# A four-layer hybrid decoder trunk on one core: order and engine of the work around the gated recurrence, and the compressed keys by token half

## The chip, the core and the metric

The program runs on one core of a Trainium2 chip. The profile names its engines PE (TensorE: matmuls; PEld is its weight load), DVE (VectorE), ACT (ScalarE), POOL (GpSimd) and SP (SyncE, which here only issues the weight DMAs). Each engine works through its own list of instructions in the order in which the built program has them; an instruction whose operands another engine makes waits on that engine. The metric is the device time of one execution in microseconds (us); the time of a kernel is the median of its runs.

## What is computed

Abridged to the two functions that the change touches. Four layers, 256 tokens of width 1024, float32. Layer 0 and 3 mix tokens by windowed attention, layer 1 by a gated linear recurrence, layer 2 by latent attention (MLA); each layer then attends to a memory and applies a gated MLP. The change touches layers 1 and 2:

```python
def rglru_block(x, w_in, conv_w, conv_b, w_rgate, b_rgate, w_igate, b_igate, lam, w_o):
    gate, u = jnp.split(x @ w_in, 2, axis=-1)
    u = causal_depthwise_conv(u, conv_w, conv_b)
    r = sigmoid(blockwise(u, w_rgate) + b_rgate)
    i = sigmoid(blockwise(u, w_igate) + b_igate)
    log_a = -LRU_C * r * softplus(-lam)
    a = jnp.exp(log_a)
    b_in = jnp.sqrt(-jnp.expm1(2.0 * log_a)) * (i * u)
    h = scan(h[t] = a[t] * h[t-1] + b_in[t])
    return (h * jax.nn.gelu(gate)) @ w_o

def mla_attention(x, w_down, q_norm, kv_norm, w_uq, w_ukv, w_o, cos_r, sin_r):
    c = x @ w_down
    cq, ckv, k_rope = jnp.split(c, [384, 640], axis=-1)
    cq, ckv = rms_norm(cq, q_norm), rms_norm(ckv, kv_norm)
    ...
```

## The kernel before

**Precision.** Every float32 product of a projection is made of three matmuls: `hi*hi + hi*lo + lo*hi` (`mm3`). So each weight piece has to be split on the chip: ACT casts a 128x512 part of the raw piece to `whi` (L287), then `wlo = raw - whi` is subtracted on DVE (L288). A piece is up to 128x2048, in parts of 512 columns, four parts to a full piece. `Weights` keeps three raw pieces (their 1 MB DMAs are issued by SP) and four split ones; `tick`, called from `bulk` after each matmul, issues a split every 1200 ns of matmul time, so that splits of later pieces lie beside the matmuls of earlier ones. Activations are split in the same way by `split` (L377 on ACT, L378 on DVE).

**Order.** A token string such as `RG_SEQ` says in which order the pieces of a layer are written; `play` walks it. In `rglru` the channels stand in four blocks of 256. Per block `b`: `a`/`b` project u, `V` is the convolution (L1173 on ACT, L1175 on DVE, tile `uc`) and the split into `uu`, `A` the two gate products and their tanh and exp (tiles `tt`, `av`, `ti`), `R` a product on DVE (L852), `g`/`h` project the gate. `Z` is one square root over `tt` of all four blocks on ACT (L885, 128x2048). `E` is the recurrence: a product (L856) and two scans of 128x256 (L858), all on DVE. `Y` is GELU on ACT (L863), its product with the state on DVE (L864), and the split into `oh`, `ol`. `C` is one chunk of the output projection: twelve matmuls of 512 columns on the four banks `y`, two chunks to a block; `G` loads the norm's weights through POOL's DMA queue into slots that `uu` leaves. `finish` makes the last four chunks, one output bank after the other, and the norm between them; the transposes of its result (`turn`, L366) and the splits `xh`, `xl` feed the next layer part.

The strings give the order of writing; the final order on each engine is made by the tile framework's scheduler, which takes the written order as priority and puts what it takes to be ready first. `tc.issue_after(ins)` lets an instruction stand no earlier than `ins`; `tc.high_priority()` lifts what is written inside.

**MLA.** `a_phase` projects the 384 query columns of both token halves (`s`), and through `more` the first half (512 of 1024 input rows) of the 320 key columns (`pk[s]`). `D` (`dk`) adds the second half of the input rows, `M` (`rms`) normalises (0, 1: queries of half 0, 1; 2, 3: keys), `U` (`c_turn`) transposes `cn` and splits it to `cqh`, `cql`.

Of the kernel before, what the change touches and what calls it, by code (L numbers as in the profile page):

```python
# [33 lines left out]
for _i in range(DEPTH):  # L34
    PHASES += [(("swa", "rglru", "mla")[_i % 3], _i), ("cross", _i), ("ffn", _i)]
SWA_SEQ = ("Q0 R0 Q1 R1 K0 U0 A2 S0 U1 B2 R2 S1 A3 N0 U2 B3 R3 N1 T0 S2 P0 U3 T1 S3 P1 C0 N2 C1 W0 T2 N3 C2 P2 T3 D3 "
           "P3 E3 G0")
RG_SEQ = ("a2 t0 b2 V1 a3 V0 V2 b3 A1 V3 g0 h0 A2 g2 A0 g1 A3 R3 R2 R0 R1 h1 Z0 E0 g3 E1 h3 Y0 C0 G0 h2 E2 E3 "
          "C1 Y1 C2 Y2 Y3 W0 C3")
MLA_SEQ = ("D1 M1 U0 M2 f1 M3 Q0 U1 K0 q0 f0 k0 v0 n0 q1 n2 v3 v1 r0 v2 n1 r1 S0 n3 S2 f2 N0 N1 f3 T0 T1 S4 N2 N3 P0 P1 G0 T2 "  # L40
           "T3 S6 N4 N5 P2 P3 T4 C0 T5 W0 N6 C1 P4 N7 T6 P5 C2 T7 P6 C3 P7")
X_SEQ = ("a2 t0 L1 b2 L0 L2 S0 a3 S1 N0 S2 T0 G0 N1 b3 T1 N2 P0 T2 L3 S3 N3 P1 W0 C0 C1 P2 T3 C2 P3 C3")

# [198 lines left out]
class Weights:  # L242


    def __init__(self, tc, pool, w):
        self.tc, self.nc, self.pool, self.w = tc, tc.nc, pool, w
        self.after = ()
        self.n_dma = self.n_split = self.n_done = 0
        self.part = 0
        self.raw, self.tiles, self.done, self.uses, self.late = {}, {}, set(), {}, []  # L250
        self.ns = 0.0
        self.hold = False
        self.then = {}

    def load(self):
# [15 lines left out]
    def step(self):  # L271
        k = self.n_split
        if k >= len(PLAN) or k - self.n_done >= NSPLIT:
            return False
        while self.n_dma <= k:
            self.load()
        n = PLAN[k][1]
        if self.part == 0:
            self.tiles[k] = (self.pool.tile([P, 2048], F32R, tag="whi", name="whi", bufs=NSPLIT),
                             self.pool.tile([P, 2048], F32R, tag="wlo", name="wlo", bufs=NSPLIT))  # L280
        hi, lo = self.tiles[k]
        c = slice(self.part, FIRST[k][self.part] if k < len(FIRST) else min(n, self.part + PART))
        raw = self.raw[k]
        with ExitStack() as st:
            for ins in self.after:
                st.enter_context(self.tc.issue_after(ins))
            self.nc.scalar.copy(out=hi[:, c], in_=raw[:, c])  # L287
            self.nc.vector.tensor_tensor(out=lo[:, c], in0=raw[:, c], in1=hi[:, c].bitcast(F32), op=ALU.subtract)  # L288
        self.part = c.stop
        if self.part >= n:  # L290
            self.part = 0
            del self.raw[k]
            self.n_split += 1
            self.load()
        return True
# [46 lines left out]
def trunk(ctx, tc, x_in, xT_in, memT_in, w, par, con, sinks, ln_g, ln_b, out):  # L342
    nc = tc.nc
    V, A, T = nc.vector, nc.scalar, nc.tensor
# [65 lines left out]
    def xs(kc, s=slice(0, 2)):  # L410
        return xh[:, s, kc], xl[:, s, kc]
# [401 lines left out]
    def rglru(mx, i, rest):  # L813
# [39 lines left out]

        def recur(b):
            t = tt[:, b]
            V.tensor_tensor(out=t, in0=t, in1=us[b][0], op=ALU.mult)  # L856
            for c in range(2):
                V.tensor_tensor_scan(out=t[:, c], data0=av[:, b, c], data1=t[:, c], initial=0.0, op0=ALU.mult, op1=ALU.add)  # L858

        def gated(b):  # L860
            ge = mx.tile([P, 2, S], F32, tag="ti", name="ge", bufs=2)
            with tc.issue_after(sq[0]):
                last[0] = A.activation(out=ge, in_=pgs.pop(b), func=AF.Gelu_apprx_tanh)  # L863
            V.tensor_tensor(out=ge, in0=ge, in1=tt[:, b], op=ALU.mult)  # L864
            oh = mx.tile([P, 2, S], F32R, tag="oh", name="oh", bufs=3)
            ol = mx.tile([P, 2, S], F32R, tag="ol", name="ol", bufs=3)
            split(oh, ol, ge)
            acts[b] = [(oh[:, c], ol[:, c]) for c in range(2)]

        op = OutProj(("mo", i), KC)  # L870
        pus, us, pgs, acts, last, sq, norm = {}, {}, {}, {}, [None], [None], [None]
        go = a_turn(mx, a_phase(("ua", i), 512, rest))

        def turned(_):
# [7 lines left out]
            return f  # L882

        def root(_):
            sq[0] = ins_of(A.activation(out=tt, in_=tt, func=AF.Sqrt, scale=0.25))  # L885

        def gb(_):
            norm[0] = Norm(op.y, mx, "uu", 3, i, 0)
# [2 lines left out]
                      "g": proj("ga", 0, pgs), "h": proj("ga", 1, pgs), "R": rate, "Z": root, "E": recur, "Y": gated,  # L891
                      "C": lambda ci: op.chunk(ci, acts[ci // 2][ci % 2]), "G": gb, "W": lambda _: want_sqrt(last[0])})
        norm[0].y = op.y
        return op.finish(acts[2] + acts[3], norm[0])


    def mla(mx, i, rest):
# [28 lines left out]
        pk = pcs[1]  # L926
# [381 lines left out]
```

## Time and profile before

| | before |
|---|---|
| time, median of 3 runs | 1379.81 us (1378.87 to 1380.73) |
| the profiled execution: its own time | 1378.62 us |
| the profiled execution: span from first to last instruction | 1376.8 us |
| PE busy, share of the span | 1362.9 us, 99% |
| DVE / ACT / POOL busy | 1084.4 / 881.4 / 13.0 us |
| granted TensorE clock, mean | 0.999 of full speed |

The window of layer 1's recurrence is about 386 to 475 us of the span, that of the head of MLA about 710 to 735 us. A row of the timeline reads: start in us, length in us, engine, line, operation, tiles out<-in, shapes, count, and in brackets the idle time of the engine just before it and what ended that. Matmuls overlap: one of 256 columns lasts 0.28 us in the rows and the next starts about 0.12 us after it; one of 512 columns lasts 0.39 and the next starts 0.23 us after it. So lost PE time is read from starts, not from lengths.

### The profile page before, as it was taken

The numbers are of one execution on the slowest core, as the hardware profiler recorded it, in microseconds if no ns is written. First come the engines' busy times: TensorE is split into PE (matmuls) and PEld (weight loads), VectorE is DVE, ScalarE is ACT, GpSimd is POOL, SyncE is SP. The second block draws the span as 40 slices with busy tenths as digits, with TensorE's granted clock in tenths as the row PEclk, the third lists the DMA queues.
The fourth block names the chain that finished last, engine by engine and source line by source line (L and its number), as shares of the span: only waits on it lengthen the run. The fifth ranks groups of instructions, "written<-read, shape, count | busy, mean of one in ns | idle before, by whom it ended". The sixth has DMA issues, their size and how long they took to land.

```text
span 1376.8 us, 23811 instructions
## 1 busy us (share of the span) xinstructions
PE 1362.9 (99%) x9122; PEld 1231.5 (89%) x9122; DVE 1084.4 (79%) x2397; ACT 881.4 (64%) x1896; POOL 13.0 (1%) x28
## 2 busy tenths in 40 slices
PE   9999999999999999999999999999999999999997
PEld 7987989999898898999988898999998879899996
DVE  6896879777888868877788686977779977897775
ACT  6675757555589667655557674855565866675553
POOL 0000000000000000000000000000000000000000
PEclk9999999999999999999999999999999999999999
DMA  9733536555435554555526442555554326455540
GB/s 334 278 118 123 214 130 237 184 187 191 174 137 197 202 175 177 214 187 194 186 86 237 154 181 95 218 211 191 191 196 145 136 109 228 153 214 189 189 174 31
DMA packets 40449, 246.78 MB, mean 179 GB/s; under 512 B 4496, under 2 KB 6800, under 8 KB 13712
## 3 DMA queue, kind: packets, MB, share of 16 engines
q1 hardware_dynamic: 36736, 232.56, 46.1%
q0 software_dynamic: 3456, 12.58, 2.7%
q8 instruction: 71, 1.16, 0.3%
q14 instruction: 42, 0.34, 0.1%
q10 hardware_dynamic: 144, 0.13, 0.0%
HBM read 244.21 MB, written 1.05 MB: 178 GB/s over the span
## 4 chain that ended last, share of the span: by engine, by line
PE 95%; DVE 3%; ACT 2%; DMA 0%; issue 0%; SPq 0%; DVEq 0%; ACTq 0%
PE ps L359 90%; PE ps L366 4%; PE ps L645 1%; ACT p L754 1%; DMA raw<-in_w_dram 0%; DVE wlo L288 0%; DVE tt L858 0%; DVE p L745 0%; DVE x L485 0%; ACT whi L287 0%; DVE x L487 0%; DVE x L461 0%; DVE tt L856 0%; ACT tt L885 0%; ACT xh L377 0%
## 5 line engine op out<-in xcount | busy, mean ns | idle before, releaser
L288 DVE TENSOR_TENSOR wlo<-raw,whi 128x512 fp32r<-128x512 f32 (+1 forms) x870 | 559.6, 683 | 144.6 <-ACT whi L287 138.1
L287 ACT CAST whi<-raw 128x512 fp32r<-128x512 f32 (+1 forms) x870 | 486.1, 619 | 165.3 <-PE ps L359 145.6
L359 PE MATMUL ps<-xh,whi 128*128 128x256 f32 x1504 | 421.2, 280 | 0.0
L359 PE MATMUL ps<-xh,wlo 128*128 128x256 f32 x1504 | 420.1, 279 | 0.0
L359 PE MATMUL ps<-xl,whi 128*128 128x256 f32 x1504 | 419.8, 279 | 0.0
L359 PEld LDWEIGHTS ps<-xl,whi 128*128 128x128 f32 x1504 | 282.7, 188 | 1.9
L359 PEld LDWEIGHTS ps<-xh,whi 128*128 128x128 f32 x1504 | 282.7, 188 | 1.8
L359 PEld LDWEIGHTS ps<-xh,wlo 128*128 128x128 f32 x1504 | 282.6, 188 | 0.0
L1175 DVE SCALAR_TENSOR_TENSOR cv<-ps,part,cv 128x255 f32<-128x255 f32 (+1 forms) x352 | 166.4, 477 | 3.8 <-ACT cv L1173 1.4
L359 PE MATMUL ps<-whi,xh 128*128 128x512 f32 (+3 forms) x336 | 118.8, 354 | 0.4 <-ACT xh L377 0.2
L359 PE MATMUL ps<-wlo,gh 128*128 128x512 f32 x352 | 116.0, 396 | 0.0
L359 PE MATMUL ps<-whi,gh 128*128 128x512 f32 x352 | 115.9, 396 | 0.0
L359 PE MATMUL ps<-wlo,xh 128*128 128x512 f32 (+3 forms) x336 | 115.7, 345 | 0.0
L359 PE MATMUL ps<-whi,gl 128*128 128x512 f32 x352 | 115.1, 393 | 0.0
L1173 ACT ACTIVATE cv<-ps,part 128x256 f32<-128x256 f32 x176 | 98.3, 563 | 16.9 <-DVE cv L1175 5.5
L377 ACT CAST gh<-cv 128x256 fp32r<-128x256 f32 x88 | 35.7, 406 | 107.6 <-DVE cv L1190 107.6
L359 PE MATMUL ps<-whi,oh 128*128 128x512 f32 x256 | 92.8, 402 | 1.9 <-ACT oh L377 1.9
L359 PE MATMUL ps<-whi,xl 128*128 128x512 f32 (+3 forms) x336 | 92.6, 347 | 0.0
L359 PE MATMUL ps<-whi,ol 128*128 128x512 f32 x256 | 90.6, 394 | 0.0
L359 PE MATMUL ps<-wlo,oh 128*128 128x512 f32 x256 | 90.2, 393 | 0.0
L359 PEld LDWEIGHTS ps<-whi,gl 128*128 128x128 f32 x352 | 66.3, 188 | 15.8
L359 PEld LDWEIGHTS ps<-wlo,gh 128*128 128x128 f32 x352 | 66.4, 189 | 15.3
(230 smaller groups left out, 1843.1 us busy)
## 6 DMA issues: line engine op xcount, KB each, us to landing
raw<-in_w_dram SPq DMA_DIRECT2D x208, 1024.0 KB, 4.8
lng<-in_ln_g_dram POOLq DMA_DIRECT2D x12, 512.0 KB, 4.0
lnb<-in_ln_b_dram POOLq DMA_DIRECT2D x12, 512.0 KB, 5.7
raw<-in_w_dram SPq DMA_DIRECT2D x15, 256.0 KB, 5.4
raw<-in_w_dram SPq DMA_DIRECT2D x5, 768.0 KB, 4.2
raw<-in_w_dram SPq DMA_DIRECT2D x2, 640.0 KB, 4.2
xf<-in_xT_dram SPq DMA_DIRECT2D x1, 1024.0 KB, 8.8
x<-in_x_dram SPq DMA_DIRECT2D x1, 1024.0 KB, 15.3
```

The costliest lines, as they stand in the source:

```text
L287: self.nc.scalar.copy(out=hi[:, c], in_=raw[:, c])
L288: self.nc.vector.tensor_tensor(out=lo[:, c], in0=raw[:, c], in1=hi[:, c].bitcast(F32), op=ALU.subtract)
L359: T.matmul(o, lhsT=l, rhs=r, start=st, stop=sp, **kw)
L366: T.transpose(o, i, ident)
L377: a = A.copy(out=hi, in_=src)
L645: T.matmul(o, lhsT=l, rhs=r, start=st, stop=sp, skip_group_check=True)
L754: last[0] = A.activation(out=pr[:, hd], in_=pr[:, hd], func=AF.Exp, scale=A_D ** -0.5, bias=nm[:, b, hd:hd + 1], accum_out=sm[:, b, hd:hd ...
L1173: A.activation(out=dst, in_=src, func=AF.Identity, scale=wc[:, taps - 1:taps], bias=bias)
L1175: V.scalar_tensor_tensor(out=dst[:, d:], in0=src[:, :S - d], scalar=wc[:, taps - 1 - d:taps - d], in1=dst[:, d:], op0=ALU.mult, op1=ALU.add)
```

## The change

1. `RG_SEQ`: `Z` stands before the four `R` instead of behind them, `Y0` right behind `E0`, `Y1` behind `E1`.
2. `recur` for blocks 0 and 1, `gated` for blocks 0 and 1 and the square root are written inside `tc.high_priority()`; and the product that begins `recur(b)` may not stand before the product of `gated(b - 1)` (for blocks 2 and 3: of `gated(1)`).
3. While `W.spare` is set (from the first token of the recurrence's string to its last), the subtraction of the second and the fourth part of a weight piece is issued to POOL instead of DVE. These are 20 subtractions of ten pieces.
4. `MLA_SEQ`: `D1` (both token halves) becomes `D0` before the transposes of the queries and `D1` behind them; `dk(s)` does one token half.

```diff
-RG_SEQ = ("a2 t0 b2 V1 a3 V0 V2 b3 A1 V3 g0 h0 A2 g2 A0 g1 A3 R3 R2 R0 R1 h1 Z0 E0 g3 E1 h3 Y0 C0 G0 h2 E2 E3 "
-          "C1 Y1 C2 Y2 Y3 W0 C3")
-MLA_SEQ = ("D1 M1 U0 M2 f1 M3 Q0 U1 K0 q0 ...
+RG_SEQ = ("a2 t0 b2 V1 a3 V0 V2 b3 A1 V3 g0 h0 A2 g2 A0 g1 A3 Z0 R3 R2 R0 R1 h1 E0 Y0 g3 E1 h3 Y1 C0 G0 h2 E2 E3 "
+          "C1 C2 Y2 Y3 W0 C3")
+MLA_SEQ = ("M1 D0 U0 M2 D1 f1 M3 Q0 U1 K0 q0 ...
...
-            self.nc.vector.tensor_tensor(out=lo[:, c], in0=raw[:, c], in1=hi[:, c].bitcast(F32), op=ALU.subtract)
+            eng = self.nc.gpsimd if self.spare and c.start in (512, 1536) else self.nc.vector
+            eng.tensor_tensor(out=lo[:, c], in0=raw[:, c], in1=hi[:, c].bitcast(F32), op=ALU.subtract)
...
         def recur(b):
             t = tt[:, b]
-            V.tensor_tensor(out=t, in0=t, in1=us[b][0], op=ALU.mult)
-            for c in range(2):
-                V.tensor_tensor_scan(...)
+            with ExitStack() as hp:
+                if b < 2:
+                    hp.enter_context(tc.high_priority())
+                with ExitStack() as st:
+                    if b:
+                        st.enter_context(tc.issue_after(gm[min(b - 1, 1)]))
+                    V.tensor_tensor(out=t, in0=t, in1=us[b][0], op=ALU.mult)
+                for c in range(2):
+                    V.tensor_tensor_scan(...)
...
+            with ExitStack() as st:
+                if b < 2:
+                    st.enter_context(tc.high_priority())
...
+                gm[b] = ins_of(V.tensor_tensor(out=ge, in0=ge, in1=tt[:, b], op=ALU.mult))
...
         def root(_):
-            sq[0] = ins_of(A.activation(out=tt, in_=tt, func=AF.Sqrt, scale=0.25))
+            with tc.high_priority():
+                sq[0] = ins_of(A.activation(out=tt, in_=tt, func=AF.Sqrt, scale=0.25))
...
-        def dk(_):
+        def dk(s):
             wt = W.get((("dk", i), 1))
             for k in range(4):
-                for s in range(2):
-                    mm3(pk[s][:, :nk], xs(4 + k, s), [t[:, nk * k:nk * k + nk] for t in wt], False, k == 3, bulk)
-            W.free((("dk", i), 1))
+                mm3(pk[s][:, :nk], xs(4 + k, s), [t[:, nk * k:nk * k + nk] for t in wt], False, k == 3, bulk)
+            if s == 1:
+                W.free((("dk", i), 1))
```

How the instructions then stand, at three places.

**Place 1, ACT and DVE, from the last gates of the recurrence (`ti_4797`, block 3) on.** On ACT, before, the four weight casts stand ahead of the square root:

```order
L847 ACTIVATE ti_4797<-ps_4784,hb_76 128x256 x2
L287 CAST whi_4806<-raw_4654 128x512 x4
L885 ACT_TABLE_LOAD
L885 ACTIVATE tt_4236<-tt_4236 128x2048
L863 ACT_TABLE_LOAD
L863 ACTIVATE ge_4897<-ps_4546 128x512
L287 CAST whi_4957<-raw_4727 128x512 x3
L377 CAST oh_4900<-ge_4897 128x512
```

The second tanh and the casts are done when the square root's table load begins. On ACT now, from the first of the two tanh of that block:

```order
L849 ACTIVATE ti_4797<-ps_4784,hb_76 128x256
L898 ACT_TABLE_LOAD
L898 ACTIVATE tt_4236<-tt_4236 128x2048
L874 ACT_TABLE_LOAD
L874 ACTIVATE ge_4845<-ps_4546 128x512
L849 ACTIVATE ti_4797<-ps_4784,hb_76 128x256
L288 CAST whi_4807<-raw_4654 128x512
L379 CAST oh_4848<-ge_4845 128x512
L288 CAST whi_4807<-raw_4654 128x512 x2
L874 ACTIVATE ge_4904<-ps_4716 128x512
```

The square root has moved ahead of the second tanh and of four weight casts (`whi_4806` before, `whi_4807` now: the weights of the first output chunks); these casts now stand behind the first GELU. On DVE, before, from the first product of the recurrence:

```order
L856 TENSOR_TENSOR tt_4236<-tt_4236,uc_4434 128x512
L856 TENSOR_TENSOR tt_4236<-tt_4236,uc_4393 128x512
L858 SCALAR_TENSOR_TENSOR tt_4236<-av_4237,tt_4236 128x256 x4
L864 TENSOR_TENSOR ge_4897<-ge_4897,tt_4236 128x512
L856 TENSOR_TENSOR tt_4236<-tt_4236,uc_4446 128x512
L856 TENSOR_TENSOR tt_4236<-tt_4236,uc_4534 128x512
L378 TENSOR_TENSOR ol_4901<-ge_4897,oh_4900 128x512
L858 SCALAR_TENSOR_TENSOR tt_4236<-av_4237,tt_4236 128x256 x4
L288 TENSOR_TENSOR wlo_4958<-raw_4727,whi_4957 128x512 x3
L864 TENSOR_TENSOR ge_4976<-ge_4976,tt_4236 128x512
```

Two blocks go step by step together, four scans in a row. On DVE now, from the same product:

```order
L864 TENSOR_TENSOR tt_4236<-tt_4236,uc_4434 128x512
L866 SCALAR_TENSOR_TENSOR tt_4236<-av_4237,tt_4236 128x256 x2
L875 TENSOR_TENSOR ge_4845<-ge_4845,tt_4236 128x512
L864 TENSOR_TENSOR tt_4236<-tt_4236,uc_4393 128x512
L850 SCALAR_TENSOR_TENSOR uc_4534<-ti_4797,uc_4534 128x512
L866 SCALAR_TENSOR_TENSOR tt_4236<-av_4237,tt_4236 128x256 x2
L380 TENSOR_TENSOR ol_4849<-ge_4845,oh_4848 128x512
L875 TENSOR_TENSOR ge_4904<-ge_4904,tt_4236 128x512
L854 SCALAR_TENSOR_TENSOR uc_4534<-av_4237,uc_4534 128x512
L290 TENSOR_TENSOR wlo_4808<-raw_4654,whi_4807 128x512
L380 TENSOR_TENSOR ol_4908<-ge_4904,oh_4907 128x512
L290 TENSOR_TENSOR wlo_4808<-raw_4654,whi_4807 128x512
```

Blocks 0 and 1 now run one after the other to their `ol`, blocks 2 and 3 behind them, and the first `wlo_4808` stands behind both, where before its like (`wlo_4807`) stood ahead of the chain.

**Place 2, PE, the first output chunk** (`oh`, `ol` are the activations, `ps_4649` is the gate projection of the third block, `h2`, 24 matmuls). On PE before, the last three of `h2` and the first of the chunk:

```order
L359 MATMUL ps_4649<-xh_69,whi_4616 128x256
L359 MATMUL ps_4649<-xl_70,whi_4616 128x256
L359 MATMUL ps_4649<-xh_69,wlo_4617 128x256
L359 MATMUL ps_4904<-whi_4806,oh_4900 128x512
L359 MATMUL ps_4905<-whi_4806,oh_4900 128x512
L359 MATMUL ps_4904<-wlo_4807,oh_4900 128x512
```

All of `h2` stands ahead of the chunk. On PE now, behind the last matmul of block 3's gate projection:

```order
L361 MATMUL ps_4911<-whi_4807,oh_4848 128x512
L361 MATMUL ps_4912<-whi_4807,oh_4848 128x512
L361 MATMUL ps_4913<-whi_4807,oh_4848 128x512
L361 MATMUL ps_4914<-whi_4807,oh_4848 128x512
L361 MATMUL ps_4912<-wlo_4808,oh_4848 128x512
L361 MATMUL ps_4914<-wlo_4808,oh_4848 128x512
L361 MATMUL ps_4649<-xh_69,whi_4616 128x256
L361 MATMUL ps_4912<-whi_4807,ol_4849 128x512
L361 MATMUL ps_4914<-whi_4807,ol_4849 128x512
```

The first chunk's twelve matmuls have moved ahead of the 24 of `h2` and stand among them; the first four take the first two parts of `whi_4807`, the fifth the second part of `wlo_4808`, which POOL makes.

**Place 3, PE, the head of MLA** (`ps_7912`, `ps_7984`: the key columns of token half 0 and 1; `cn_7875` the normalised queries). On PE before, the last product of half 1 and what follows:

```order
L359 MATMUL ps_7984<-whi_7959,xh_69 128x320
L359 MATMUL ps_7984<-wlo_7960,xh_69 128x320
L359 MATMUL ps_7984<-whi_7959,xl_70 128x320
L366 MATMUL ps_8048<-cont_64,cn_7875 128x128 x2
L366 MATMUL ps_8053<-cont_64,cn_7875 128x128 x2
L366 MATMUL ps_8058<-cont_64,cn_7875 128x128 x2
L359 MATMUL ps_8072<-cqh_7870,whi_8002 128x256
```

No matmul stands between the transposes and the first that needs their result. On PE now, from the eighth product of half 1 (the same three transposes for token half 0 stand ahead of half 1's first):

```order
L361 MATMUL ps_7984<-whi_7959,xh_69 128x320
L361 MATMUL ps_7984<-wlo_7960,xh_69 128x320
L368 MATMUL ps_8032<-cont_64,cn_7875 128x128
L368 MATMUL ps_8037<-cont_64,cn_7875 128x128
L368 MATMUL ps_8042<-cont_64,cn_7875 128x128
L361 MATMUL ps_7984<-whi_7959,xl_70 128x320
L361 MATMUL ps_7984<-whi_7959,xh_69 128x320
L361 MATMUL ps_7984<-wlo_7960,xh_69 128x320
L361 MATMUL ps_7984<-whi_7959,xl_70 128x320
L361 MATMUL ps_8072<-cqh_7870,whi_8011 128x256
```

Four matmuls of half 1 now stand between the transposes of the queries and the first matmul that takes their result.

## Rows read from the trace of the kernel before

**Rows 1.** The page: the span, and busy time of each engine.
```profile
span 1376.8 us, 23811 instructions
PE 1362.9 (99%) x9122; PEld 1231.5 (89%) x9122; DVE 1084.4 (79%) x2397; ACT 881.4 (64%) x1896; POOL 13.0 (1%) x28
```
**Rows 2.** Stretches: PE, PEld, DVE, ACT, POOL busy (count), clock, DMA share, GB/s.
```profile
434.00:440.00 6.00, 4.80 (x29) 4.03 (x28) 6.00 (x12) 5.17 (x11) 0.00 (x0) 1.00 0.09 40
440.00:446.00 6.00, 5.29 (x22) 3.74 (x21) 6.00 (x12) 4.53 (x9) 0.00 (x0) 1.00 0.19 57
```
**Rows 3.** Timeline of PE, end of the projections to the second block's chunk.
```profile
435.66 0.28 PE L359 MATMUL ps<-xh,wlo 128*128 128x256 f32 x1
437.14 0.73 PE L359 MATMUL ps<-whi,oh 128*128 128x512 f32 x2 [1.20 <-ACT oh L377]
...
442.35 0.62 PE L359 MATMUL ps<-whi,ol 128*128 128x512 f32 x2
443.68 0.73 PE L359 MATMUL ps<-whi,oh 128*128 128x512 f32 x2 [0.71 <-ACT oh L377]
```
**Rows 4.** Timeline of ACT around the square root.
```profile
426.06 0.82 ACT L847 ACTIVATE ti<-ps,hb 128x256 f32<-128x256 f32 x2
426.77 2.17 ACT L287 CAST whi<-raw 128x512 fp32r<-128x512 f32 x4
428.96 1.28 ACT L885 ACT_TABLE_LOAD   x1
430.26 1.92 ACT L885 ACTIVATE tt<-tt 128x2048 f32<-128x2048 f32 x1
...
433.49 0.60 ACT L863 ACTIVATE ge<-ps 128x512 f32<-128x512 f32 x1
...
436.47 0.62 ACT L377 CAST oh<-ge 128x512 fp32r<-128x512 f32 x1 [0.83 <-DVE ge L864]
```
**Rows 5.** Timeline of DVE, the recurrence.
```profile
432.21 1.29 DVE L856 TENSOR_TENSOR tt<-tt,uc 128x512 f32<-128x512 f32 x2 [1.60 <-ACT tt L885]
433.42 2.43 DVE L858 TENSOR_TENSOR_SCAN tt<-av,tt 128x256 f32<-128x256 f32 x4
435.77 0.66 DVE L864 TENSOR_TENSOR ge<-ge,tt 128x512 f32<-128x512 f32 x1
...
440.50 1.87 DVE L288 TENSOR_TENSOR wlo<-raw,whi 128x512 fp32r<-128x512 f32 x3
```
**Rows 6.** The chain that ended last, norm after the recurrence: start, length, what.
```profile
461.44 0.59 ACT xh L377
...
467.95 0.60 ACT xh L377
```
**Rows 7.** Timeline of ACT, then of PE: the head of MLA.
```profile
728.02 1.21 ACT L946 ACTIVATE cqh<-ps,part 128x256 fp32r<-128x256 f32 x3
...
727.38 0.82 PE L366 MATMUL ps<-cont,cn 128*128 128x128 f32 x6
728.55 0.39 PE L359 MATMUL ps<-cqh,whi 128*128 128x256 f32 x1 [0.35 <-ACT cqh L946]
```
**Rows 8.** DVE by groups, 390 to 450 us: count, busy us, mean ns, idle before.
```profile
L288 DVE TENSOR_TENSOR wlo<-raw,whi 128x512 fp32r<-128x512 f32 x41 | 26.3, 682 | 0.0
...
L858 DVE TENSOR_TENSOR_SCAN tt<-av,tt 128x256 f32<-128x256 f32 x8 | 4.9, 668 | 0.0
```
**Rows 9.** Timeline of POOL, 380 to 450 us: all that it does there.
```profile
413.74 0.53 POOL L450 DMA_DIRECT2D lng<-in_ln_g_dram  x1 [216.90 <-PE ps L359]
419.39 0.53 POOL L451 DMA_DIRECT2D lnb<-in_ln_b_dram  x1 [5.12 <-PE ps L359]
```
**Rows 10.** Timeline of DVE, then of PE: convolution, `uu`, and the gate product that takes it.
```profile
394.34 2.50 DVE L1175 SCALAR_TENSOR_TENSOR uc<-ps,part,uc 128x255 f32<-128x255 f32 x6 [0.41 <-ACT uc L1173]
...
400.83 1.29 DVE L378 TENSOR_TENSOR uu<-uc,uu 128x512 fp32r<-128x512 f32 x2
...
401.95 0.41 PE L359 MATMUL ps<-uu,whi 128*128 128x256 f32 x2
```

More of the change, by code (lines that the diff above doesn't have):

```diff
@@ L37 @@
            "P3 E3 G0")
-RG_SEQ = ("a2 t0 b2 V1 a3 V0 V2 b3 A1 V3 g0 h0 A2 g2 A0 g1 A3 R3 R2 R0 R1 h1 Z0 E0 g3 E1 h3 Y0 C0 G0 h2 E2 E3 "
-          "C1 Y1 C2 Y2 Y3 W0 C3")
-MLA_SEQ = ("D1 M1 U0 M2 f1 M3 Q0 U1 K0 q0 f0 k0 v0 n0 q1 n2 v3 v1 r0 v2 n1 r1 S0 n3 S2 f2 N0 N1 f3 T0 T1 S4 N2 N3 P0 P1 G0 T2 "
+RG_SEQ = ("a2 t0 b2 V1 a3 V0 V2 b3 A1 V3 g0 h0 A2 g2 A0 g1 A3 Z0 R3 R2 R0 R1 h1 E0 Y0 g3 E1 h3 Y1 C0 G0 h2 E2 E3 "
+          "C1 C2 Y2 Y3 W0 C3")
+MLA_SEQ = ("M1 D0 U0 M2 D1 f1 M3 Q0 U1 K0 q0 f0 k0 v0 n0 q1 n2 v3 v1 r0 v2 n1 r1 S0 n3 S2 f2 N0 N1 f3 T0 T1 S4 N2 N3 P0 P1 G0 T2 "
            "T3 S6 N4 N5 P2 P3 T4 C0 T5 W0 N6 C1 P4 N7 T6 P5 C2 T7 P6 C3 P7")
@@ L252, in __init__ @@
         self.hold = False
+        self.spare = False
         self.then = {}
@@ L855, in recur @@
             t = tt[:, b]
-            V.tensor_tensor(out=t, in0=t, in1=us[b][0], op=ALU.mult)
-            for c in range(2):
-                V.tensor_tensor_scan(out=t[:, c], data0=av[:, b, c], data1=t[:, c], initial=0.0, op0=ALU.mult, op1=ALU.add)
+            with ExitStack() as hp:
[6 more added lines that the diff above has]
+                for c in range(2):
+                    V.tensor_tensor_scan(out=t[:, c], data0=av[:, b, c], data1=t[:, c], initial=0.0, op0=ALU.mult, op1=ALU.add)
         def gated(b):
             ge = mx.tile([P, 2, S], F32, tag="ti", name="ge", bufs=2)
[L862 to L867, printed above, removed]
+            with ExitStack() as st:
+                if b < 2:
+                    st.enter_context(tc.high_priority())
+                with tc.issue_after(sq[0]):
+                    last[0] = A.activation(out=ge, in_=pgs.pop(b), func=AF.Gelu_apprx_tanh)
+                gm[b] = ins_of(V.tensor_tensor(out=ge, in0=ge, in1=tt[:, b], op=ALU.mult))
+                oh = mx.tile([P, 2, S], F32R, tag="oh", name="oh", bufs=3)
+                ol = mx.tile([P, 2, S], F32R, tag="ol", name="ol", bufs=3)
+                split(oh, ol, ge)
             acts[b] = [(oh[:, c], ol[:, c]) for c in range(2)]
+        W.spare = True
         op = OutProj(("mo", i), KC)
-        pus, us, pgs, acts, last, sq, norm = {}, {}, {}, {}, [None], [None], [None]
+        pus, us, pgs, acts, gm, last, sq, norm = {}, {}, {}, {}, {}, [None], [None], [None]
         go = a_turn(mx, a_phase(("ua", i), 512, rest))
@@ L893, in rglru @@
         norm[0].y = op.y
+        W.spare = False
         return op.finish(acts[2] + acts[3], norm[0])
```

## The prediction

> **What bounds the kernel now.** I read the page first: PE is busy for 1362.9 of 1376.8 us [rows 1], so almost nothing can be won by making anything faster; only the few places where PE waits count. The stretches show one such place in the recurrence: the two from 434 on, 6.00 us each, hold PE busy for 4.80 and 5.29 us while DVE is busy for all 6.00 of both [rows 2]. The PE timeline gives the waits there. The last matmul of the projections starts at 435.66 and takes 0.12 to the next start, but the first output chunk starts at 437.14: 1.36 us lost. At 442.35 two matmuls of 0.23 stand, the next starts at 443.68: 0.87 lost. Both wait for ACT's cast `oh` [rows 3]. Before the cast stands this chain. ACT ends the last tanh at 426.88, does four weight casts until 428.94, loads a table, and takes the root from 430.26 to 432.18 [rows 4]; DVE, idle for 1.60 us until then, does two products and four scans and reaches the product with the GELU at 435.77 [rows 5]; ACT casts it from 436.47 to 437.09 [rows 4]. So 2.2 us of PE are lost behind 2.1 us of casts, 0.6 of a product and 1.2 of scans that block 0 and 1 do not need for their first chunk.
>
> Two smaller places: the norm after the recurrence, where the chain that ended last leaves PE twice for the cast `xh`, 0.59 and 0.60 us [rows 6], and the head of MLA, where PE ends six transposes at 728.20 and waits 0.35 us for `cqh`, which ACT starts at 728.02 [rows 7].
>
> **Part 1, the priorities and the order (first chunk).** I lay the new order out with durations of the old rows. ACT: after the first tanh (half of 0.82) at 426.5 the table load (1.28) to 427.8, the root (1.92) to 429.7, the second load to 431.0, the GELU (0.60) to 431.6, the other tanh to 432.0, one weight cast (a quarter of 2.17) to 432.5 [rows 4]. DVE: one product (start to start 0.60) to 430.3, two scans of 0.60 to 431.5, the wait for the GELU until 431.6, the gated product to 432.3 [rows 5]. ACT casts `oh` from 432.5 to 433.1. That is 4.0 us earlier than before.
>
> PE does not get all of it, since it also comes earlier: 24 matmuls of `h2` that stood ahead of the chunk now stand behind its first six, 24 x 0.117 = 2.8, so PE arrives at 435.78 - 2.8 = 433.0. It then meets four waits. `oh` at 433.1: 0.15 with the signal. The second part of `whi`, cast right behind `oh`, at 433.65: 0.25. The second part of `wlo`, which POOL can only start then: done at 434.4 to 435.1 (prices below), where PE arrives at 434.35: 0 to 0.7. `ol`, which DVE reaches after the product (432.9), the step that follows it (433.5) and two scans (434.7), at 435.3: it takes over where POOL was quick. Sum 1.05, at either price of POOL about the same. From there 11 matmuls of `h2` cover the first `wlo` that DVE makes (437.1, PE 437.3), and 12 more the rest. The second block's `oh` is due at 436.5 and needed at 442. So 2.2 lost becomes 1.05: **-1.2**. Bounds: -2.2 if all of it is covered, +0.5 if POOL's part comes 1.7 us later than laid out.
>
> What is late next is the norm: its subtractions now stand earlier on DVE, no longer between its steps, and PE reaches it 1.2 us earlier. The two casts [rows 6] cost PE 0 to 0.6 us each; I take back half, **-0.5**, bounds 0 and -0.9.
>
> **Part 2, half of the subtractions on POOL.** DVE gives away 20 subtractions; one costs it 0.60 from start to start (three in 1.87, of which the last takes 0.68) [rows 5], together 12 us. No row shows an arithmetic instruction on POOL. From below I bound one by DVE's own, 0.68; from above by the slowest DVE step per column in this phase, the scan, 0.668 for 256 columns, so 1.34 for 512 [rows 8]. I take 1.34: POOL has not been shown to be quick at anything. At 1.34 twenty take 26.8 of about 60 us, so POOL keeps up by itself. ACT casts a pair of parts in 1.08, so at the start of the phase POOL falls behind by 0.26 a pair; over the six pairs before the convolution 1.6 us, and the first matmul on such a part comes a whole projection later than its cast: no cost.
>
> POOL's queue is no longer empty. The two norm loads stood there and waited for PE until 413.74 and 419.39 [rows 9]; now a second part of one piece waits behind the first, and one piece behind the second. The weights concerned are those of the gate projections from 419 and from 427 on; the subtractions can start at 414.3 and 420 and are done 5 us before PE needs them. Cost 0. SP's 1 MB loads wait for the last reader of a raw piece, now POOL: at most 0.7 later (1.34 against 0.68), against three pieces in flight: 0.
>
> The Trainium skill has a price: GPSIMD Engine Reference, section 3.1, gives 1.96 times DVE's time for a two-input addition of 2048 columns; an estimate by that page is 1.96 x 0.682 = 1.34 us, which leaves the sum as it is. No run here shows it yet.
>
> **Part 3, MLA.** The same instructions; four matmuls of 0.147 now stand behind the transposes, 0.6 us, and cover ACT's cast. The transposes of the second half need the normalised queries about 0.4 us earlier than before; ACT has two weight casts fewer ahead of their squares, 1.1 us. **-0.4**, bounds -0.6 and +0.3.
>
> **The sum:** -1.2 - 0.5 - 0.4 = -2.1, so 1378.6 becomes 1376.5 for an execution like the profiled one. The median of the runs stands 1.2 above that execution, and the forecast is for a median: 1379.8 - 2.1 = **1377.7**. Its own range, from the bounds that can hold together, is -3.7 to +0.2: 1376.1 to 1380.0.
>
> **Rival 1, slower: POOL and DVE take turns.** Nearly everything DVE does here reads two operands from SBUF. If a subtraction on POOL and such an instruction can't run side by side, DVE gives 0.60 away and gets p, POOL's price, back as a wait. Where it decides: before the convolution DVE did twelve subtractions, 7.2 us, and 0.41 of idle; now it does seven and stands still for six of POOL's, 4.2 + 6p. The convolution, at 394.34 before [rows 10], begins at 390.9 + 6p. It reads PSUM and one SBUF operand and runs on beside POOL; with one subtraction fewer in it, the first `uu` is split 6.5 us later, at 397.4 + 6p. PE takes it at 402.07, the second matmul from 401.95 [rows 10]. So PE stands from p = 0.77 on. At 1.34 the split comes at 405.4 and PE loses 3.4 us. At the first chunk one or two of POOL's turns fall into DVE's chain: the 1.2 of part 1 is gone, and up to 1.4 more. Sum: 3.4 + (0 to 1.4) - 0.9 = +2.5 to +3.9; with p = 0.77 it is +0.5, with turns in the later pieces too +5.5. I give +3: 1382.8. For it: DVE is at 6.00 of 6.00 where this falls. Against: no row shows POOL and DVE at work together, and the trace has only POOL's two DMA issues in this phase. The rule stands in the Trainium skill, SBUF — State Buffer, section "Who interferes with whom": a DVE instruction with two SBUF inputs contends with a GpSimd instruction that reads SBUF, and the later one waits for the whole of the other. By that rule the change would come out slower, as worked out here.
>
> **Rival 2, the wait only changes its name.** PE comes to the chunk 2.8 us earlier and finds the weights' second part, which POOL can start only after ACT's cast, 2 us later than laid out; then -1.2 is +0.8, the norm gains nothing, and with MLA the time is about 1379.8. For it: four new waits within 1.5 us, all without slack. Against: even then the `h2` matmuls stand behind as cover for all that follows.
>
> **Rival 3, all of it is covered:** -2.2 - 0.9 - 0.6 = -3.7, 1376.1. It is the lower end of the forecast's own range. Against: the `ol` of block 0 ends 0.7 us after PE's arrival by every price.
>
> **How the numbers follow.** A measurement of this kernel can tell about 0.2%, 2.8 us, from no change. The forecast with rival 3 at its end has 0.52: 0.18 for a gain over 2.8, 0.34 within. Rival 2 has 0.12, all within. Rival 1 has 0.36, two thirds of it above +2.8: 0.24, and 0.12 within. So faster 0.18, same 0.58, slower 0.24. The range begins at 1375.9, 0.2 below rival 3, with some 0.05 left out, and ends at 1384.0, +4.2, which leaves out the upper part of rival 1, about 0.10.
>
> **What would show it.** The table load of the root behind one tanh and not behind four casts; its end near 429.7; `oh` near 433; PE's wait for `oh` under 0.3 us, and new ones for a `wlo` of POOL's and for `ol`, of 1 us together. Rival 1: DVE subtractions or scans that last 1 us and more where POOL runs, and an idle PE at the first gate product near 402. Rival 2: waits of PE for POOL alone of 1 us and more at the chunk. At the head of MLA PE should not wait for `cqh`. The prediction would be wrong if POOL's subtraction takes over 2 us alone, or if PE stops anywhere before 430.

## The result, and the profile after

The changed kernel takes 1386.36 us (median of 6 runs, 1385.36 to 1387.98), the kernel before in the same session 1379.59 us: a ratio of 1.0051, 95% interval 1.0041 to 1.0061. It is 6.8 us slower, where 2.1 us less was forecast, and beyond the upper end of the range, 1384.0. The profiled executions differ by as much: the page of the changed kernel [rows 1 for before].

```profile
span 1383.8 us, 23844 instructions
PE 1365.0 (99%) x9122; PEld 1232.9 (89%) x9122; DVE 1088.5 (79%) x2375; ACT 882.0 (64%) x1896; POOL 46.6 (3%) x50
```

DVE has 22 instructions fewer and POOL 22 more (eleven pieces, two parts each; the sections ahead count 20 of ten). Yet DVE is busy for 4.1 us longer. The timeline of POOL, DVE and PE up to the first gate product says why (columns as in the rows before; in time order within each engine):

```profile
387.08 9.87 POOL L290 TENSOR_TENSOR wlo<-raw,whi 128x512 fp32r<-128x512 f32 x6 [190.26 <-ACT whi L288]
...
401.15 2.52 POOL L290 TENSOR_TENSOR wlo<-raw,whi 128x512 fp32r<-128x512 f32 x2 [1.23 <-issue]
...
387.55 9.95 DVE L290 TENSOR_TENSOR wlo<-raw,whi 128x512 fp32r<-128x512 f32 x6 [0.27 <-ACT whi L288]
...
400.75 2.80 DVE L1189 SCALAR_TENSOR_TENSOR uc<-ps,part,uc 128x255 f32<-128x255 f32 x7
403.52 1.30 DVE L380 TENSOR_TENSOR uu<-uc,uu 128x512 fp32r<-128x512 f32 x2
...
401.81 0.28 PE L361 MATMUL ps<-xh,wlo 128*128 128x256 f32 x1
403.54 0.39 PE L361 MATMUL ps<-uu,whi 128*128 128x256 f32 x1 [1.45 <-ACT uu L379]
404.27 0.38 PE L361 MATMUL ps<-uu,whi 128*128 128x256 f32 x1 [0.34 <-DVE uu L380]
```

Six subtractions take DVE 9.95 us beside six of POOL's in 9.87: the two engines take turns. Beside the convolution (L1189, which reads PSUM and one operand from SBUF) DVE keeps its pace of 0.40 a step, and POOL's two subtractions take 2.52, 1.25 each. So the split of `uu`, and with it PE's first gate product, comes late: from 401.81 to 403.54 and on to 404.27, less 0.12 for each matmul, PE loses 1.61 + 0.61 = 2.2 us where it lost nothing before.

The second place is behind the first output chunk. POOL, DVE and PE again:

```profile
441.84 5.06 POOL L290 TENSOR_TENSOR wlo<-raw,whi 128x512 fp32r<-128x512 f32 x3 [2.46 <-issue]
447.69 1.42 POOL L290 TENSOR_TENSOR wlo<-raw,whi 128x512 fp32r<-128x512 f32 x1 [0.79 <-ACT whi L288]
...
442.26 1.78 DVE L290 TENSOR_TENSOR wlo<-raw,whi 128x512 fp32r<-128x512 f32 x1
443.97 3.47 DVE L864 TENSOR_TENSOR tt<-tt,uc 128x512 f32<-128x512 f32 x2
447.37 3.44 DVE L866 TENSOR_TENSOR_SCAN tt<-av,tt 128x256 f32<-128x256 f32 x4
450.74 2.47 DVE L290 TENSOR_TENSOR wlo<-raw,whi 128x512 fp32r<-128x512 f32 x4
...
437.82 0.73 PE L361 MATMUL ps<-wlo,oh 128*128 128x512 f32 x2 [0.74 <-POOL wlo L290]
...
439.99 0.73 PE L361 MATMUL ps<-whi,ol 128*128 128x512 f32 x2 [1.31 <-DVE ol L380]
...
447.01 0.63 PE L361 MATMUL ps<-whi,oh 128*128 128x512 f32 x2
451.45 1.20 PE L361 MATMUL ps<-wlo,oh 128*128 128x512 f32 x2 [3.81 <-DVE wlo L290]
...
454.98 0.63 PE L361 MATMUL ps<-whi,ol 128*128 128x512 f32 x2
```

A subtraction, two products and four scans, 4.2 us of work by the rows of before, last from 442.26 to 450.74, 8.5 us: four of POOL's turns lie in them. Only then comes the subtraction that PE has waited for since 447.5: 451.45 - 447.01 - 2 x 0.23 = 3.98 us lost. And behind this wait PE is slow for a while: the eight matmuls from 451.45 to 454.98 take 3.53 us from start to start, not 8 x 0.23 = 1.84. The stretches (length, busy time of PE, PEld, DVE, ACT, POOL with counts, granted clock, DMA share, GB/s) show why: from 451.4 to 455.0 the granted clock is 0.53 and 0.52, the lower of its two levels (1.2 of 2.4 GHz), and then full again:

```profile
402.00:408.00 6.00, 4.21 (x33) 3.92 (x33) 6.00 (x15) 5.16 (x10) 3.00 (x3) 1.00 0.40 162
...
451.40:453.30 1.90, 1.85 (x4) 1.47 (x5) 1.90 (x4) 0.00 (x0) 0.00 (x0) 0.53 0.15 34
453.30:455.00 1.70, 1.70 (x6) 1.34 (x5) 1.70 (x4) 1.12 (x2) 0.00 (x0) 0.52 0.90 352
455.00:457.00 2.00, 2.00 (x10) 1.64 (x9) 2.00 (x5) 1.16 (x3) 0.00 (x0) 1.00 0.71 274
```

| PE time lost, us, from starts of matmuls (all gaps over 0.1) | before | after | difference |
|---|---|---|---|
| first gate products, ~402 | 0 | 2.3 | +2.3 |
| first chunk and the wait for the second `oh` | 2.7 | 3.3 | +0.6 |
| the wait at 447 | 0 | 4.0 | +4.0 |
| the eight matmuls behind it | 0 | 1.7 | +1.7 |
| the norm behind the recurrence | 0.9 | 0 | -0.9 |
| the wait at the head of MLA | 0.6 | 0 | -0.6 |

The sum is +7.1; the spans differ by 7.0. For the runs below it helps to count between the same two matmuls on either side of the recurrence: from the start of PE's 2660th, the last ahead of the gate products, to that of its 3151st, behind the norm. That takes 77.76 us before and 85.40 after, 7.6 more.

### The profile page after: what moved, and what is told of

It is laid out like the page before. It is cut to its first block, busy times and chain, and to the rows that moved or that the text cites. A ratio compares the mean times of both kernels' runs of the same rounds, so it can differ in the third digit from the quotient of the medians.

```text
span 1383.8 us, 23844 instructions
## 1 busy us (share of the span) xinstructions
PE 1365.0 (99%) x9122; PEld 1232.9 (89%) x9122; DVE 1088.5 (79%) x2375; ACT 882.0 (64%) x1896; POOL 46.6 (3%) x50
## 3 DMA queue, kind: packets, MB, share of 16 engines
HBM read 244.21 MB, written 1.05 MB: 177 GB/s over the span
## 4 chain that ended last, share of the span: by engine, by line
PE 93%; DVE 4%; ACT 2%; issue 0%; DMA 0%; DVEq 0%; SPq 0%; ACTq 0%
PE ps L361 88%; PE ps L368 4%; PE ps L647 2%; DVE wlo L290 1%; ACT p L756 1%; DVE tt L866 0%; DVE uc L1189 0%; ACT whi L288 0%; DVE tt L864 0%; DMA raw<-in_w_dram 0%; DVE p L747 0%; DVE x L487 0%; DVE x L489 0%; DVE x L463 0%; ACT tt L898 0%
## 5 line engine op out<-in xcount | busy, mean ns | idle before, releaser
L1189 DVE SCALAR_TENSOR_TENSOR cv<-ps,part,cv 128x255 f32<-128x255 f32 (+1 forms) x352 | 166.2, 477 | 3.8 <-ACT cv L1187 1.4
```

The lines of the kernel that those rows point to most:

```text
L1189: V.scalar_tensor_tensor(out=dst[:, d:], in0=src[:, :S - d], scalar=wc[:, taps - 1 - d:taps - d], in1=dst[:, d:], op0=ALU.mult, op1=ALU.add)
```

## The experiments

All ratios are to the kernel before, measured on the same chip. Theory T was formed from the rows above: turns between POOL and DVE are what makes the change slow.

| kernel | median, us | ratio, 95% interval |
|---|---|---|
| 1. changed, nothing on POOL | 1379.34 | 1.0000, 0.9991 to 1.0009 |
| 2. before, with subtractions on POOL | 1386.02 | 1.0048, 1.0035 to 1.0060 |
| 3. before, with the MLA part | 1378.89 | 0.9996, 0.9987 to 1.0005 |
| 4. as 1, and POOL subtracting beside it for nobody | 1392.44 | 1.0096, 1.0082 to 1.0109 |
| 5. changed, POOL's first 12 only | 1382.46 | 1.0023, 1.0013 to 1.0033 |
| 6. changed, POOL's last ten only | 1383.80 | 1.0035, 1.0021 to 1.0048 |
| 7. as 4, but copies | 1382.03 | 1.0024, 1.0014 to 1.0035 |
| 8. as 1, two subtractions on POOL at the norm | 1381.40 | 1.0015, 1.0006 to 1.0024 |
| 9. as 4, but writes only | 1379.51 | 1.0003, 0.9992 to 1.0013 |
| 10. 3, with eight weight casts on POOL | 1376.95 | 0.9984, 0.9975 to 0.9992 |
| 11. 3, with four of them | 1378.75 | 0.9996, 0.9988 to 1.0005 |
| 12. 1, with eight weight casts on POOL | 1377.14 | 0.9984, 0.9975 to 0.9993 |

### 1 to 3: which part costs

Run 1:

```diff
-        W.spare = True
...
-        W.spare = False
```

> The changed kernel with all subtractions back on DVE; priorities, order and MLA part stay. Theory T (a POOL subtraction and a DVE instruction with two SBUF operands take turns, and that alone makes the change slow): no PE stall near 402 us, every DVE product and subtraction lasts 0.7 us again, the wait of 3.98 us at 447.2 is gone or under 1 us, and what part 1, the norm and part 3 were to bring is left: 1377 to 1378.5. Rival O (the new DVE order by itself puts block 1's products and scans ahead of the subtraction that PE waits for at 447.2): the stall near 402 goes (2.2 us), but 2 to 4 us stay at 447, and the time is 1381 to 1384.

Run 2, on the kernel before:

```diff
-            self.nc.vector.tensor_tensor(out=lo[:, c], in0=raw[:, c], in1=hi[:, c].bitcast(F32), op=ALU.subtract)
+            eng = self.nc.gpsimd if self.spare and c.start in (512, 1536) else self.nc.vector
+            eng.tensor_tensor(out=lo[:, c], in0=raw[:, c], in1=hi[:, c].bitcast(F32), op=ALU.subtract)
```

> The kernel before with half of the subtractions of the recurrence on POOL, and nothing else. T: DVE subtractions before 397 start 1.7 us apart instead of 0.6, PE stalls by 2 to 2.5 us near 402, and the chain to the first chunk at 435 gets some turns more: +3 to +6, 1383 to 1386. O: with the old order POOL does no harm: 1379 to 1380.5.

Run 3, on the kernel before, is item 4 of the change alone.

> The kernel before with the MLA part alone. Both theories: the wait for cqh at 728.5 is gone, -0.3 to -0.6 us, 1379.1.

POOL's part alone makes all of the loss (+6.7 in run 2); the rest of the change brings nothing (0.0 in run 1). T is right on the cause; the time of run 1 lies above its 1377 to 1378.5 and below rival O's 1381 to 1384. ACT and PE of run 1 in the recurrence, PE in the norm:

```profile
427.24 1.92 ACT L897 ACTIVATE tt<-tt 128x2048 f32<-128x2048 f32 x1
...
432.02 0.62 ACT L379 CAST oh<-ge 128x512 fp32r<-128x512 f32 x1
...
432.28 0.28 PE L361 MATMUL ps<-xh,wlo 128*128 128x256 f32 x1
432.70 1.48 PE L361 MATMUL ps<-whi,oh 128*128 128x512 f32 x4
...
436.82 0.50 PE L361 MATMUL ps<-wlo,oh 128*128 128x512 f32 x1 [0.30 <-DVE wlo L290]
...
443.36 0.50 PE L361 MATMUL ps<-wlo,oh 128*128 128x512 f32 x1 [0.65 <-DVE wlo L290]
...
468.61 0.50 PE L361 MATMUL ps<-whi,xh 128*128 128x512 f32 x1 [0.67 <-ACT xh L379]
```

From the chain of the kernel before that ended last:

```profile
468.59 1.20 PE ps L359 x4
```

The chain of run 1 is as early as laid out, and yet at 468.61 PE starts the very matmul that before starts at 468.59, though run 1 came to the gate products 0.58 us earlier (401.37, before 401.95 [rows 10]). So the new order by itself costs the recurrence 0.6 us (78.35 to 77.76 between the two matmuls named above), and the MLA part gives 0.4 of it back. The reason stands in DVE's subtractions by stretch. Before (length, DVE busy and count, clock, DMA share, GB/s):

```profile
420.00:432.00 12.00, 5.06 (x8) 1.00 0.59 225
432.00:470.00 38.00, 12.81 (x20) 1.00 0.45 164
```

Run 1:

```profile
420.00:432.00 12.00, 2.49 (x4) 1.00 0.53 197
432.00:470.00 38.00, 15.32 (x24) 1.00 0.46 166
```

The early root displaces four of ACT's weight casts, DVE has nothing to subtract meanwhile and stands idle, and the four subtractions come back in the stretch in which it has no time. What PE gains at the chunk it gives back, and more, at 443.36 and at the norm, where it waits for what DVE does last. Run 3 takes the wait for `cqh` away (its first matmul starts 0.20 us behind the one ahead of it), but its 0.4 us are less than its interval can show.

In run 2 the clock falls behind the first stall already. The stretch of it (columns as in the stretches above):

```profile
402.00:408.00 6.00, 4.21 (x25) 3.81 (x24) 6.00 (x15) 5.17 (x9) 3.82 (x3) 0.82 0.50 182
```

### 4, 7 and 9: what takes turns

All three start from the changed kernel. DVE does every subtraction itself, and POOL works on raw weights that are no longer needed; no engine waits for its result, only the next load of the buffer does. Run 4:

```diff
+            self.nc.vector.tensor_tensor(out=lo[:, c], in0=raw[:, c], in1=hi[:, c].bitcast(F32), op=ALU.subtract)
+            if self.spare and c.start in (512, 1536):
+                self.nc.gpsimd.tensor_tensor(out=raw[:, c], in0=raw[:, c], in1=hi[:, c].bitcast(F32), op=ALU.subtract)
```

> The changed kernel with all 40 subtractions of the phase on DVE, and POOL doing 20 subtractions more over raw weights that nobody reads again; no matmul waits for POOL, only the next load of the buffer does. T: up to 20 turns of 1.1 us in DVE's queue with all of DVE's own work in it: the stall near 402 is 4 us or more, and the time 6 to 14 us above the kernel without POOL's work. If instead the late results of POOL were what cost (rival L: DVE is slow only because of waits on data), DVE's instructions keep 0.6 us from start to start, and the time is that of the kernel without POOL's work within 1 us.

Run 7 has `tensor_copy(out=raw[:, c], in_=raw[:, c])` in its last line, run 9 `memset(raw[:, c], 0.0)`.

> As the kernel with POOL's work beside DVE's (all subtractions on DVE, nobody waits for POOL), but POOL's 20 instructions are copies with one operand from SBUF instead of subtractions with two. Theory R (it is enough that POOL reads SBUF at all): DVE's instructions with two SBUF operands start 1 us and more apart next to it, PE stalls at 402 as with the two-operand form, scaled by the length of a copy; 1384 to 1392. Rival B (both engines must take two): DVE keeps 0.6 us from start to start and the time is 1379 to 1380.

> As the two runs with POOL's work beside DVE's (all subtractions on DVE, nobody waits for POOL), but POOL's instructions read nothing: they write zeros over raw weights that are no longer needed. Theory R (it is POOL's reading of SBUF that takes the turn): DVE's subtractions start 0.60 us apart next to it, no stall at 402, 1379 to 1380, the time without POOL's work. Rival W (any access of POOL takes it, writing too): DVE's neighbours last 1 us and more as beside the copies; 1381 to 1383.

DVE's subtractions before the convolution and one POOL instruction of each. Run 4:

```profile
387.78 10.48 DVE L289 TENSOR_TENSOR wlo<-raw,whi 128x512 fp32r<-128x512 f32 x10
...
391.44 1.68 POOL L291 TENSOR_TENSOR raw<-raw,whi 128x512 f32<-128x512 f32 x1 [0.63 <-DVE wlo L289]
```

Run 7:

```profile
386.37 9.38 DVE L289 TENSOR_TENSOR wlo<-raw,whi 128x512 fp32r<-128x512 f32 x12
...
389.34 1.01 POOL L291 COPY raw<-raw 128x512 f32<-128x512 f32 x1 [0.60 <-DVE wlo L289]
```

Run 9:

```profile
386.57 7.31 DVE L289 TENSOR_TENSOR wlo<-raw,whi 128x512 fp32r<-128x512 f32 x12
...
389.12 0.53 POOL L291 MEMSET raw<- 128x512 f32 x1 [0.68 <-DVE wlo L289]
```

Twelve subtractions without company take 0.69 + 11 x 0.60 = 7.3 us, ten 6.1. So one turn costs DVE (10.48 - 6.1) / 4 = 1.10 us beside a two-operand POOL instruction (four lie in the stretch), (9.38 - 7.3) / 5 = 0.42 beside a one-operand copy, and nothing beside a write. The writes cost nothing elsewhere either: run 9 takes 78.36 us between the two matmuls named above, run 1 78.35. Late results are not the cause (rival L), for nobody waits for any here; and POOL's copies suffice: beside one, two of DVE's subtractions start 0.60 + 0.42 = 1.02 us apart, as theory R said, but the time, 1382.03, is below its 1384 to 1392. The Trainium skill states this in SBUF — State Buffer, section "Who interferes with whom": a DVE instruction with two inputs in SBUF contends with a GpSimd instruction that reads SBUF, not with one that only writes it. The three runs agree, 1.10, 0.42 and 0.00 us.

### 5 and 6: early or late

```diff
-            eng = self.nc.gpsimd if self.spare and c.start in (512, 1536) else self.nc.vector
+            turn = self.spare and c.start in (512, 1536)
+            if turn and self.k0 is None:
+                self.k0 = k
+            eng = self.nc.gpsimd if turn and k - self.k0 < 6 else self.nc.vector
```

Run 6 has `>= 6`.

> The changed kernel with POOL's share cut to its first 12 subtractions (the six pieces up to the gate projections); the other ten are DVE's again. Theory T (each turn costs where it falls): the stalls near 402 stay, 2.2 us together; behind them the recurrence runs as without POOL, with 0.5 us before the wlo matmuls of the first chunk and 0.8 at the next, and no wait of 4 us. 1381 to 1383, the upper end if PE's clock drops after the stall. Rival I (inherited: DVE's debt from before 402 is what makes the late 4 us): the long wait at 447 stays and the time is that of the changed kernel, 1386.

> The changed kernel with POOL's share cut to its last ten subtractions, from 414 on. T: no stall near 402; the three instructions of POOL's next to block 1's products and scans cost 1.1 us each, so the waits of 0.9 and 1.5 us in the first chunk and of 4 us behind it stay, 1.3 us more from the lower clock after it; the norm's waits are gone. 1383 to 1385. Rival I: without the debt from 402 the late waits are 1 us together, 1379 to 1380.

Each half brings its own loss, +3.4 and +4.7 us by the medians. These add up to more than the whole, +6.8. In the traces they add up: between the two matmuls named above run 5 takes 80.65 us and run 6 83.01, 2.3 and 4.7 more than run 1, and the changed kernel 7.05 more. The profiled execution of run 5, 1380.55, is the shortest of its nine; what makes the others longer is in no trace. PE's waits from 400 to 480 in run 6 (who waited for whom: us in total, times, longest):

```profile
PE ps L364 <- DVE wlo L293: 3.8, 1, 3.8
PE ps L364 <- DVE ol L383: 1.3, 1, 1.3
PE ps L364 <- POOL wlo L293: 0.7, 1, 0.7
```

These are the late waits of the changed kernel, to the tenth, without its early ones; run 5 has the early ones, 1.5 and 0.3, and the late ones of run 1. Rival I is out: nothing is inherited from 402.

### 8: two subtractions where DVE reads PSUM

```diff
+            beside = PLAN[k][0] == (("xqa", 1), 1) and c.start >= 1024
+            eng = self.nc.gpsimd if beside else self.nc.vector
```

> The kernel without POOL's share (all on DVE) with just two subtractions on POOL, those of the last two parts of the second piece of the next projection, at the place where DVE runs the norm's second half: there most of DVE's neighbours read PSUM. T: beside an instruction that reads PSUM no turn is taken, DVE gives 1.2 us away in the one stretch where PE waits for it, and the waits of 0.84 and 0.35 us in the norm go down to under 0.4 together: 1378.3 to 1378.9. Rival: the two fall next to the norm's two-operand steps or come late for the matmuls that read them, and the time is 1379.3 to 1380.5.

It is the rival's case, and worse than it said. POOL, DVE and PE of run 8:

```profile
456.83 3.50 POOL L291 TENSOR_TENSOR wlo<-raw,whi 128x512 fp32r<-128x512 f32 x2 [36.83 <-DVE mv L470]
...
457.63 1.56 DVE L488 SCALAR_TENSOR_TENSOR x<-x,mv,lng 128x512 f32<-128x512 f32 x1
459.11 1.25 DVE L481 SCALAR_TENSOR_TENSOR mv<-mv 128x1 f32<-128x1 f32 x1
...
462.39 1.38 PE L369 MATMUL ps<-cont,x 128*128 128x128 f32 x8 [1.76 <-DVE x L490]
```

POOL has no other work, so it starts as soon as the casts are there, 5 us earlier than DVE did these two, and meets the first half's two-operand steps. Even the norm's step of one column, 0.20 us otherwise, takes 1.25. PE loses 1.92 us at the transposes (460.24 to 462.39, less 0.23). The profiled execution, 1379.99, is one of five of 1379.09 to 1380.76 us with a mean granted clock of 0.998 or 0.999; the other six, 1381.40 to 1382.49, have 0.997, which would fit a fall of the clock behind this wait but is not shown by a trace. The place of a POOL instruction is set by its inputs, not by where DVE would have done it.

### 10 to 12: the casts on POOL instead

After run 1, theory D: DVE's two-operand work behind the root is the limit, and DVE idles ahead of the root because ACT, full with tanh and exp, casts too little. A cast has one operand, costs ACT 0.52 us, and a turn beside it 0.42 to a DVE that is idle anyway. Run 10 is run 3 with

```diff
-            self.nc.scalar.copy(out=hi[:, c], in_=raw[:, c])
+            if self.spare and self.k0 is None:
+                self.k0 = k
+            if self.spare and k - self.k0 in (7, 8):
+                self.nc.gpsimd.tensor_copy(out=hi[:, c], in_=raw[:, c])
+            else:
+                self.nc.scalar.copy(out=hi[:, c], in_=raw[:, c])
```

Run 11 has `(7,)`; run 12 is run 1 with the edit of run 10.

> The kernel before with the MLA part, all subtractions on DVE in the old order, and the eight weight casts that stand on ACT before the root (two pieces) on POOL instead: one operand, and beside a DVE that is idle for 4.6 us from 420 to 432. Theory D (what limits this place is DVE's stock of two-operand work behind the root, and DVE waits before it because ACT is full): the root ends 2 to 4 us earlier, the first chunk's waits of 1.36 and 0.87 us go down to under 0.5 together, the norm gains up to 0.5; with 0.4 of MLA -2 to -3 us: 1376 to 1377.3. Rival C (POOL's casts come late or their turns of 0.42 us hit DVE, or the weights are late for PE): 1379 to 1382.

> As the run with eight casts on POOL, but only the four of the first of the two pieces. D: half of the gain, the root 2 us earlier, 1377 to 1378. C: 1379 to 1380.5.

> The changed kernel with all subtractions on DVE, and with the same eight weight casts on POOL. D: the root 2 us earlier than in the run without POOL's share, DVE does the subtractions of these pieces before 432 and not behind the root, the norm's waits of 1.7 us and the chunk's of 1.9 shrink by 2 us together: 1376.5 to 1377.5. If the order of the old kernel is the better one, it is behind the run with that order by up to 1 us. C: 1379 to 1382.

Runs 10 and 12 beat both kernels, by 2.1 and 1.9 us to the kernel before. Of this 1.8 and 1.6 come from the recurrence (75.98 and 76.18 us between the two matmuls named above, 77.76 before), the rest from the MLA part. POOL, DVE and ACT of run 12 ahead of the root:

```profile
424.60 3.21 POOL L291 CAST whi<-raw 128x512 fp32r<-128x512 f32 x4 [1.96 <-PE ps L365]
...
425.25 3.70 DVE L294 TENSOR_TENSOR wlo<-raw,whi 128x512 fp32r<-128x512 f32 x4 [0.75 <-POOL whi L291]
...
423.27 0.84 ACT L846 ACTIVATE tt<-ps,hb 128x256 f32<-128x256 f32 x2 [2.12 <-PE ps L365]
...
427.74 1.92 ACT L902 ACTIVATE tt<-tt 128x2048 f32<-128x2048 f32 x1
```

DVE's subtractions of run 12 by stretch:

```profile
420.00:432.00 12.00, 7.08 (x8) 1.00 0.73 270
432.00:470.00 38.00, 12.81 (x21) 1.00 0.41 150
```

The four subtractions are back ahead of the root, slowed by turns (7.08 us for eight), and PE's waits from 400 to 480 are down to

```profile
PE ps L365 <- DVE ol L384: 0.4, 1, 0.4
PE ps L372 <- DVE x L493: 0.3, 1, 0.3
PE ps L365 <- ACT oh L383: 0.2, 1, 0.2
```

D holds for DVE and fails for ACT: the root of run 12 is no earlier than in run 1 (427.74 to 427.24), since ACT waits 2.12 us for PE's gate products ahead of the last block's gates (L846). Run 11 shows the same: ACT waits 2.13 us at this place, its root starts at 430.48 (430.26 before) and not 2 us earlier, and the recurrence takes 77.70 us. So the first piece's casts lay in time that ACT would have waited anyway, and only the MLA part is left of its gain. In run 10 the first `oh` still costs PE 1.4 us, more than D said; what it gains in the recurrence is the second `oh` (0.87 before) and half of the norm. Whether a mixture is better yet was not tried.

## Why the prediction was wrong

**What bounds the kernel** was read rightly as to PE, and too narrowly as to DVE: the two waits for `oh` are there, but behind them stands a DVE with no time left until the norm. "DVE is busy for all 6.00 of both" was in the text as an observation and not used as a bound on part 1.

**Part 1** was laid out well and valued wrongly. In run 1 the root ends at 429.16 (429.7 laid out), `oh` at 432.64 (433.1), PE arrives at 432.4 (433.0) and loses 0.30 for `oh`, 0.29 for the second `whi` and 0.46 for `wlo`: 1.05, the sum that was given. The step that failed is "From there 11 matmuls of `h2` cover the first `wlo` that DVE makes (437.1, PE 437.3), and 12 more the rest": 0.81 us are lost at 443.36, and the norm, from which 0.5 was to come back, costs 1.0 more (PE's gaps there are 1.9 us, 0.9 before). The four weight casts were counted as time that the chain gets rid of; that their subtractions must be done later, by the engine that is late next, was not.

**Part 2** has the failed step on which the sign hangs. The price was taken as time of POOL, 1.34 us; the rows give 1.25 beside the convolution, and that was near enough. The estimate by the Trainium skill, GPSIMD Engine Reference, section 3.1, was 1.34 as well, 0.09 above these rows. The step that failed is that the cost to DVE was taken as nothing, with rival 1 at 0.36 since "no row shows POOL and DVE at work together". That the trace has no such row was used as evidence against, and it was none: nothing spoke for running side by side either, while rival 1 had a stated rule and a DVE at 6.00 of 6.00 on its side. Runs 4 and 9 show the turn in its place: at 1.10 a turn against 0.60 saved, the offload loses 0.5 us of DVE's time with each instruction that falls beside two-operand work.

**Rival 1** was the right mechanism. Its first place fits once p, which it took as POOL's price, is the turn: with p = 1.10 its own formula puts the split of `uu` at 397.4 + 6.6 = 404.0 (measured 403.52) and PE's loss at 2.0 (measured 2.2). The formula adds 6.5 us for the convolution, although the text says that there is one subtraction fewer in it; 6.09 were measured (397.43 to 403.52). The term that was mis-sized is its second: 0 to 1.4 us for turns at the first chunk, where 0.6 + 4.0 were lost. Four turns fall into the subtraction, the products and the scans of the later blocks that the new order puts ahead of the subtraction PE needs next; the text had "turns in the later pieces" at up to +5.5, which is still below the +6.8 measured, and the range cut it off at +4.2. The term that was missing is the clock: 1.7 us at the lower level behind the wait.

**Part 3** came as forecast: the wait for `cqh` is gone, 0.6 us, of which 0.2 is lost again behind it. From PE's 4501st to its 5001st matmul the changed kernel takes 80.23 us, the kernel before 80.62, so 0.4 less. In the time of run 3 it can't be told from nothing. **Rival 2** had its own piece: PE waits 0.7 for POOL's `wlo` at the chunk, less than the 1 us that would have spoken for it, and it decides nothing.

**Signs that were named**: DVE instructions of 1 us and more beside POOL, and an idle PE near 402, are both there, and are what the text gave as rival 1's. "PE stops anywhere before 430", one of its two signs of being wrong, came true at 402; the other, over 2 us for POOL's subtraction alone, did not.

## What to carry to other kernels

Before work is moved from DVE to POOL, list what DVE does meanwhile. Where its instructions read two operands from SBUF, price the move at the turn (here 1.10 us for a two-operand instruction, 0.42 for a one-operand one, per 128x512), not at POOL's spare time. In this kernel a cast was cheaper to move than a subtraction, and relieved another engine. When a wait of the critical engine is removed, ask how much work the engine behind it has left until the next place where it is waited for: an order that leaves that engine idle early gives the gain back later. A missing row is no evidence against a rival.

## What the runs showed of the hardware

- POOL's turn reaches very short DVE instructions: the step of 128x1 took 1.25 us where it takes 0.20 (run 8).
- POOL takes 1.25 us for a subtraction of 128x512 where DVE reads PSUM and one operand from SBUF (402), and 1.67 where it takes turns with DVE (run 4). Each of its writes takes 0.53, beside DVE and without cost to it (run 9).
- PE's granted clock fell to its lower level behind the wait of 4.0 us and cost 1.7 us more; a matmul of 512 columns then starts 0.43 us behind the one ahead of it, not 0.23. A wait need not end so: near 402 the same two, 1.61 and 0.61 us, are followed by a granted clock of 0.82 in run 2, and of 1.00 from 402 to 408 in the changed kernel. Why the one and not the other was not settled.
